# Second mixer: the first pair of groups attended before the compressed blocks, whose part is added later

## The chip, the cores and the metric

One core of a Trainium2 chip runs the whole program. The metric is the device time of one execution in microseconds, and the time of a kernel is the median of its runs. TensorE (PE in the rows) multiplies and transposes, VectorE (DVE) and ScalarE (ACT) work element by element, GpSimd (POOL) does a few small things, and SyncE (SP) issues nearly all transfers. Matmul results land in PSUM, which has eight banks.

## The reference

A decoder trunk of two layers on 256 tokens of width 1024, in fp32. Each layer is a mixer and a SwiGLU FFN, each behind an RMSNorm, with residual additions. The change lies in the second layer's mixer (the "odd" one, native sparse attention): 16 heads of 64 in 4 groups with a key and value head each. Every query gets three attentions, which are gated and added:

```python
s = einsum('bqghd,bngd->bqghn', qb, k_cmp) * scale          # 15 compressed blocks
o_cmp = einsum('bqghn,bngd->bqghd', safe_softmax(s, ...), v_cmp)
...                                                          # o_slc: selected blocks
...                                                          # o_win: sliding window
return g[..., 0:1] * o_cmp + g[..., 1:2] * o_slc + g[..., 2:3] * o_win
```

With 256 tokens there are four selectable blocks and all are selected, and the window of 512 reaches back to the first token, so both o_slc and o_win are causal attentions over all tokens, each with keys and values of its own. The compressed keys and values are made from overlapping stretches of 32 tokens by a small network (`compress`: a matmul over 32 x 64 inputs, a gelu, a second matmul).

## The kernel before

The 256 tokens are two tiles of 128 (t = 0, 1). Every projection is made with three matmuls per 128 rows of weights (`mm3`, lines 264 to 267): a weight tile is split into a rounded part (`w_hi`, ScalarE, line 108) and the rest (`w_lo`, VectorE, line 109), and so are the activations. The class `Weights` loads the tiles in the order of use, five raw buffers and seven split ones, and prepares them six tiles ahead of use. A chunk of w columns (`OD_CHUNKS`) is four weight tiles and 48 matmuls, and its two results take two of the four `mm` banks. The two `s` banks hold scores, and the two `tp` banks hold transposes and the attention's results.

`odd_mixer` works in this order: the chunk of 304 columns (48 gates and the compressed keys' inputs) and that of 256 (the compressed values' inputs), with rope, transposes (`pt_f`) and the sums into `flat` (lines 621 to 667). Then come two pairs of groups (`for gp in range(2)`, line 719), and for each: the queries' chunk of 512, the keys' and values' chunk of 512, their split and transposed forms `qS`, `kS`, `kX`, `vv`; the compressed softmax of both tiles (lines 744 to 768), which ends in `cT`; then for each tile the attention. `compress()` is called once, behind the first queries. The attention of a tile goes in groups: scores into an `s` bank (line 787), maximum and exponential (`softmax_terms`), reciprocal and gate (796, 797), scaling (801), transposes into a `tp` bank (806), eviction to `pT`. When all eight heads are there, one `tp` bank collects the compressed part (814) and the values (822), and `split` writes it into `oT`. Tile 0 has four groups of four scalings of 128 columns for a pair, tile 1 eight groups of two scalings of 256. The first layer of `compress` reads its weights (`cw1`) from the two `pT` buffers, so that the attention cannot write `pT` before.

`residual` is the output projection: eight weight tiles of 1024 columns, each for both tiles and halves, the last three together at the end. Rows 0 to 511 of the weights belong to the first pair, so that their matmuls can run once the first pair's `oT` is there. A norm gain is loaded by SyncE into the single `gain` tile.

The program's text gives priorities: a scheduler takes on each engine, in a simulated time, the ready instruction that stands first in the text, and the engine then runs that fixed order. `pin` holds some instructions (the SyncE queue among them) in the order of the text.

Of the kernel before, what the change touches and what calls it, by code (L numbers as in the profile page):

```python
# [28 lines left out]
OD_CHUNKS = [304, 256, 512, 512, 512, 512]  # L29
# [91 lines left out]
def trunk(tc, x, w0, w1, sm0, cw, vec, cst, out, dbg=None):  # L121
# [481 lines left out]
    def odd_mixer(nm, goff):  # L603
        aT, rs = nm.aT, nm.rs
        with tc.tile_pool(name="odd", bufs=1, reuse_waits="tile") as pool:

            def early(name):
                return pool.tile([P, D], F32, tag="aT", bufs=2 * NT, name=name)


# [10 lines left out]
            for v in range(2):  # L621
# [4 lines left out]
                ps = project(aT, OD_CHUNKS[v])  # L626
                cw1.append(pool.tile([P, 2 * D], F32, tag="pT", bufs=2, name="cw1"))
                pin(nc.sync.dma_start(cw1[v], cw[:, 2 * v * D : (2 * v + 2) * D]))
                for t in range(NT):
                    o = 0  # L630
                    if v == 0:
                        nrs = small_tile(1, "nrs")
                        gt = gates[t].rearrange("p a b c -> p (a b c)")
                        V.tensor_scalar(nrs, rs[t], -1.0, None, op0=ALU.mult)
                        A.activation(gt, ps[t][:, :48], AF.Exp, scale=nrs)
                        V.tensor_scalar(gt, gt, 1.0, None, op0=ALU.add)
                        V.reciprocal(gt, gt)
                        o = 48
                    nk = nat("nk")[:, :384].rearrange("p (a b d) -> p a b d", a=2, b=3)
                    src = ps[t][:, o : o + 256].rearrange("p (a b d) -> p a b d", a=2, b=2)  # L640
                    if v == 0:
                        for a in range(2):
                            rope(pool, nk[:, a, :2], src[:, a], rs[t], t, 2, 64)
                    else:
                        A.activation(nk[:, :, :2], src, AF.Copy, scale=rs[t])
                    V.tensor_copy(nk[:, :, 2], nk[:, :, 0])
                    pt = t_bank("pt_f").rearrange("p (k c) -> p k c", k=4)
                    for a in range(2):
                        for s in range(2):
                            TE.transpose(pt[:, 2 * a + s], nk[:, a, s : s + 2].rearrange("p b d -> p (b d)"), ident)  # L650
                    evac(F[:64, :, t * P : (t + 1) * P], pt[:64])
                    lo, hi = (1, P) if t == 0 else (0, P)
                    for s in range(2):
                        dst = F[64:].rearrange("p (a b) c -> p a b c", b=2)[:, :, 1 - s, t * P + lo - 1 : t * P + hi - 1]
                        evac(dst, pt[64:].rearrange("p (a b) c -> p a b c", b=2)[:, :, s, lo:hi])
# [12 lines left out]

            def compress():

                hp = s_bank("ps_h")[:, :P]
                for j in range(16):
                    for v in range(2):
                        mmi = TE.matmul(
                            hp[64 * v : 64 * v + 64], fls[v][:, j], cw1[v][:, j * P : (j + 1) * P], start=j == 0, stop=j == 15, skip_group_check=True
                        )
                        if j or v:
                            pin(mmi)
# [29 lines left out]
            oT = new_aT(pool)  # L708

# [9 lines left out]
            for gp in range(2):  # L719
                qS = [pool.tile([P, 8, P], F32R, tag="qS", bufs=3, name="qS") for _ in range(NT)]  # L720
                kS = pool.tile([P, 2, 2, T], F32R, tag="kS", bufs=2, name="kS")
                kX = pool.tile([P, 2, 2, T], F32R, tag="kX", bufs=2, name="kX")
                vv = pool.tile([P, NT, 256], F32, tag="vv", bufs=2, name="vv")
                ps = project(aT, 512)
                for t in range(NT):
                    nq = nat("nq").rearrange("p (b d) -> p b d", d=64)
                    rope(pool, nq, ps[t].rearrange("p (b d) -> p b d", d=64), rs[t], t, 8, 64)
                    for h0 in (0, 4):
                        evac(qS[t][:, h0 : h0 + 4], stacked(nq[:, h0 : h0 + 4], 4, "pt_q"))
                if gp == 0:  # L730
                    compress()
                ps = project(aT, 512)
                for t in range(NT):
                    nk = nat("nk")[:, :256].rearrange("p (b d) -> p b d", d=64)
                    rope(pool, nk, ps[t][:, :256].rearrange("p (b d) -> p b d", d=64), rs[t], t, 4, 64)
                    A.activation(vv[:, t], ps[t][:, 256:], AF.Copy, scale=rs[t])
                    pt = stacked(nk, 4, "pt_k").rearrange("p (b r) c -> p r b c", b=2)
                    tq = slice(t * P, (t + 1) * P)
                    evac(kS[:, :, :, tq], pt)
                    for z in range(2):  # L740
                        evac(kX[64 * z : 64 * z + 64, :, :, tq], pt[64 * (1 - z) : 64 * (1 - z) + 64])


                cTs = []
                for t in range(NT):
                    sb = s_bank("ps_c")[:, :256].rearrange("p (h z n) -> p h z n", h=8, z=2)
                    for h in range(8):
                        TE.matmul(sb[:, h].rearrange("p z n -> p (z n)"), qS[t][:, h], kcs[:, 2 * gp + h % 2].rearrange("p z n -> p (z n)"), start=True, stop=True)
                    sc = pool.tile([P, 8, 16], F32, tag="sc", bufs=1, name="sc")
                    mx = small_tile(8, "mx", 2)  # L750
                    dn = small_tile(8, "dn", 2)
                    cm = con[:, C_CMP + 16 * t : C_CMP + 16 * t + 16]
                    V.tensor_add(sc, sb[:, :, 0], cm.unsqueeze(1).broadcast_to([P, 8, 16]))
                    V.tensor_add(sc, sb[:, :, 1], sc)
                    V.tensor_reduce(mx, sc, axis=AX.X, op=ALU.max)
                    V.tensor_scalar(mx, mx, NEG / 10, None, op0=ALU.max)
                    V.tensor_tensor(sc, sc, mx.unsqueeze(2).broadcast_to([P, 8, 16]), op=ALU.subtract)
                    A.activation(sc, sc, AF.Exp, scale=64 ** -0.5)
                    V.tensor_reduce(dn, sc, axis=AX.X, op=ALU.add)
                    V.scalar_tensor_tensor(dn, dn, 0.0, dn, op0=ALU.is_equal, op1=ALU.add)  # L760
                    V.reciprocal(dn, dn)
# [207 lines left out]
```

## Time and profile before

| | us |
|---|---|
| median of 3 runs | 676.5 |
| lowest and highest run | 675.41, 676.85 |
| the profiled execution | 676.92 |
| its span, first to last instruction | 675.1 |
| TensorE busy | 651.3 (96%) |
| VectorE busy | 435.6 (65%) |
| ScalarE busy | 369.5 (55%) |
| mean DMA rate | 162 GB/s |

Times in rows are microseconds from the start of the span. A matmul's row lasts longer than the distance to the next, since matmuls are pipelined: the distance between starts is what one costs in a stream. A bracket at the end of a row tells how long the engine was idle before it and on what it had waited.

### The profile page before, as it was taken

To read this page: it belongs to the slowest core of one execution; us is meant where nothing else is said; L and a number is where in the kernel's file an instruction comes from. 1 tells how busy PE (TensorE), PEld (TensorE's weight loads), DVE (VectorE), ACT (ScalarE), POOL (GpSimd) and SP (SyncE) were. 2 spreads that over 40 slices of the span, in tenths; PEclk is the share of its full clock that TensorE was granted. 3 is DMA by queue.
4 is the path that set the end of the run, shared out by engine and by line. 5 is a ranking of instruction groups with operands and counts; after the bars stand their busy time and mean duration, and the time that the engine had idled before them with its cause. 6 is when DMAs were issued, how large, how long until landed. Compare 5 with 4: busy or idle time off the path is not lost.

```text
span 675.1 us, 9324 instructions
## 1 busy us (share of the span) xinstructions
PE 651.3 (96%) x3329; PEld 533.7 (79%) x3329; DVE 435.6 (65%) x954; ACT 369.5 (55%) x671; POOL 12.4 (2%) x24
## 2 busy tenths in 40 slices
PE   5999999999999999999999999969999999999996
PEld 4979788778888889888887877746788888898884
DVE  4989977767455555543588899696674555465424
ACT  4775847547444444433376687686574544444322
POOL 1000000100000000000000000000000000000000
PEclk9999999999999999999999999989999999999999
DMA  8845355138666666662386431400396555555501
GB/s 313 254 149 168 117 165 157 31 109 319 201 184 184 192 182 184 185 193 74 101 346 216 155 126 39 150 0 2 121 329 196 178 178 196 181 182 187 186 1 62
DMA packets 31869, 109.62 MB, mean 162 GB/s; under 512 B 3536, under 2 KB 3792, under 8 KB 31568
## 3 DMA queue, kind: packets, MB, share of 16 engines
q1 hardware_dynamic: 31392, 108.45, 49.5%
q8 instruction: 26, 0.43, 0.3%
q10 hardware_dynamic: 432, 0.59, 0.2%
q14 instruction: 19, 0.16, 0.1%
HBM read 107.98 MB, written 1.05 MB: 161 GB/s over the span
## 4 chain that ended last, share of the span: by engine, by line
PE 82%; ACT 6%; DMA 5%; DVE 4%; issue 2%; POOL 0%; SPq 0%; POOLq 0%; DVEq 0%; ACTq 0%
PE ps_out L265 7%; PE ps_out L267 7%; PE ps_out L266 7%; PE ps_g L267 5%; PE ps_g L266 5%; PE ps_g L265 5%; PE ps_u L266 5%; PE ps_u L267 5%; PE ps_u L265 5%; DMA w_raw<-in_w 5%; PE ps_in L265 4%; PE ps_in L267 4%; PE ps_in L266 4%; PE pt_a L215 3%; PE ps_o L822 2%
## 5 line engine op out<-in xcount | busy, mean ns | idle before, releaser
L109 DVE TENSOR_TENSOR w_lo<-w_raw,w_hi 128x1024 fp32r<-128x1024 f32 (+5 forms) x200 | 234.5, 1180 | 176.6 <-ACT w_hi L108 176.2
L108 ACT ACTIVATE w_hi<-w_raw 128x1024 fp32r<-128x1024 f32 (+5 forms) x200 | 202.9, 1024 | 203.4 <-PE ps_out L267 58.6
L265 PE MATMUL ps_in<-w_hi,aT 128*128 128x512 f32 (+5 forms) x208 | 77.5, 373 | 1.2 <-ACT aT L209 1.2
L267 PE MATMUL ps_in<-w_hi,aT 128*128 128x512 f32 (+5 forms) x208 | 77.2, 373 | 0.0
L266 PE MATMUL ps_in<-w_lo,aT 128*128 128x512 f32 (+5 forms) x208 | 76.7, 370 | 0.0
L265 PE MATMUL ps_g<-w_hi,aT 128*128 128x512 f32 (+1 forms) x192 | 72.4, 377 | 0.0
L267 PE MATMUL ps_g<-w_hi,aT 128*128 128x512 f32 (+1 forms) x192 | 71.8, 376 | 0.0
L266 PE MATMUL ps_g<-w_lo,aT 128*128 128x512 f32 (+1 forms) x192 | 71.7, 373 | 0.0
L265 PE MATMUL ps_u<-w_hi,aT 128*128 128x512 f32 (+1 forms) x192 | 71.3, 371 | 0.0
L266 PE MATMUL ps_u<-w_lo,aT 128*128 128x512 f32 (+1 forms) x192 | 71.3, 371 | 0.0
L267 PE MATMUL ps_u<-w_hi,aT 128*128 128x512 f32 (+1 forms) x192 | 71.3, 371 | 0.0
L265 PE MATMUL ps_out<-w_hi,hT_hi 128*128 128x512 f32 x176 | 69.5, 395 | 0.0
L267 PE MATMUL ps_out<-w_hi,hT_lo 128*128 128x512 f32 x176 | 69.3, 394 | 0.0
L266 PE MATMUL ps_out<-w_lo,hT_hi 128*128 128x512 f32 x176 | 68.5, 389 | 0.0
L265 PEld LDWEIGHTS ps_in<-w_hi,aT 128*128 128x128 f32 x208 | 39.9, 192 | 6.1 <-ACT aT L209 1.8
L320 ACT ACTIVATE e<-e,bias 128x128 f32<-128x128 f32 (+1 forms) x96 | 42.5, 446 | 3.1 <-DVE bias L319 3.0
L267 PEld LDWEIGHTS ps_in<-w_hi,aT 128*128 128x128 f32 x208 | 39.7, 191 | 4.5 <-DVE aT L210 0.3
L266 PEld LDWEIGHTS ps_in<-w_lo,aT 128*128 128x128 f32 x208 | 39.7, 191 | 4.4 <-issue 0.4
L265 PEld LDWEIGHTS ps_u<-w_hi,aT 128*128 128x128 f32 x192 | 36.2, 188 | 6.3
L266 PEld LDWEIGHTS ps_u<-w_lo,aT 128*128 128x128 f32 x192 | 36.2, 188 | 6.3
L267 PEld LDWEIGHTS ps_u<-w_hi,aT 128*128 128x128 f32 x192 | 36.2, 188 | 6.2
L265 PEld LDWEIGHTS ps_g<-w_hi,aT 128*128 128x128 f32 x192 | 36.2, 188 | 6.0
(208 smaller groups left out, 946.2 us busy)
## 6 DMA issues: line engine op xcount, KB each, us to landing
w_raw<-in_w SPq DMA_DIRECT2D x176, 512.0 KB, 3.6
w_raw<-in_w SPq DMA_DIRECT2D x8, 384.0 KB, 4.6
gain<-in_vec SPq DMA_DIRECT2D x4, 512.0 KB, 5.1
cw<-in_cw SPq DMA_DIRECT2D x2, 1024.0 KB, 8.2
w_raw<-in_w SPq DMA_DIRECT2D x4, 416.0 KB, 6.6
w_raw<-in_w SPq DMA_DIRECT2D x4, 328.0 KB, 6.9
w_raw<-in_w SPq DMA_DIRECT2D x4, 304.0 KB, 2.8
x<-in_x SPq DMA_DIRECT2D x4, 256.0 KB, 6.2
```

The source lines that it names most:

```text
L108: nc.scalar.activation(hi[:, :n], raw[:, :n], AF.Copy)
L109: nc.vector.tensor_sub(lo[:, :n], raw[:, :n], hi[:, :n])
L215: TE.transpose(pt[:, i], src[:, i * P : (i + 1) * P], ident)
L265: TE.matmul(ps, act[0][:, k], wh, start=start, stop=False)
L266: TE.matmul(ps, act[0][:, k], wl, start=False, stop=False)
L267: TE.matmul(ps, act[1][:, k], wh, start=False, stop=stop)
L320: A.activation(e, e, AF.Exp, scale=-1.0, bias=bias, accum_out=den)
L822: pin(TE.matmul(ob[64 * par : 64 * par + 64], vv[:, st, c : c + 64], pTs[par][:, b, st].rearrange("p j c -> p (j c)"), start=False, stop=l ...
```

## The change

The order of the second mixer's program is changed. The first pair's queries, keys and values are projected first. Then the chunk of 304 columns follows (`compress_inputs(0)`, with the gates), then the first pair's attention of tile 0 without its compressed part, the chunk of 256 (`compress_inputs(1)`), and the attention of tile 1. The two results are evicted to SBUF by ScalarE, into the tile of the norm gain. Then come `compress`, and for each tile the first pair's compressed softmax, its product with the compressed values in a bank of its own, an addition on VectorE and the split into `oT`. The second pair is as before. `cw1` lies in four pieces in a third `qS`, a second `kS` and `kX` and an `aT` buffer, no longer in `pT`. In tile 0 the four scalings of a group become one multiplication with a repeated operand, and in tile 1 the gate is a second factor in the scaling, so that the product of reciprocal and gate falls away. The columns on the host are reordered to match.

```diff
-OD_CHUNKS = [304, 256, 512, 512, 512, 512]
+OD_CHUNKS = [512, 512, 304, 256, 512, 512]
...
+            def compress_inputs(v):
                 F = early("F").rearrange("p (g c) -> p g c", g=4)
...
-                ps = project(aT, OD_CHUNKS[v])
-                cw1.append(pool.tile([P, 2 * D], F32, tag="pT", bufs=2, name="cw1"))
-                pin(nc.sync.dma_start(cw1[v], cw[:, 2 * v * D : (2 * v + 2) * D]))
+                ps = project(aT, OD_CHUNKS[2 + v])
+                if v == 0:
+                    tags = (("qS", 3), ("kS", 2), ("kX", 2), ("aT", 2 * NT))
+                    for i, (tag, bufs) in enumerate(tags):
+                        cw1.append(pool.tile([P, D], F32, tag=tag, bufs=bufs, name="cw1"))
+                        pin(nc.sync.dma_start(cw1[i], cw[:, i * D : (i + 1) * D]))
...
-                            cf = den[:, : 2 * g].rearrange("p (g b) -> p g b", b=2)
-                            h0 = 2 * j0 + par
-                            V.reciprocal(cf, cf)
-                            V.tensor_mul(cf, cf, gates[t][:, gp, h0 : h0 + 2 * g - 1 : 2, 1:3])
-                            for i in range(g):
-                                for b in range(2):
-                                    z = 2 * i + b
-                                    V.tensor_scalar(e[:, i, b], e[:, i, b], den[:, z : z + 1], None, op0=ALU.mult)
+                        h0 = 2 * j0 + par
+                        V.reciprocal(den[:, : 2 * g], den[:, : 2 * g])
+                        if t:
+                            for b in range(2):
+                                V.tensor_scalar(e[:, 0, b], e[:, 0, b], den[:, b : b + 1], gates[t][:, p.gp, h0, 1 + b : 2 + b], op0=ALU.mult, op1=ALU.mult)
+                        else:
+                            cf = den.rearrange("p (g b) -> p g b", b=2)
+                            V.tensor_mul(cf, cf, gates[t][:, p.gp, h0 : h0 + 2 * g - 1 : 2, 1:3])
+                            V.tensor_mul(e, e, cf.unsqueeze(3).broadcast_to([P, g, 2, ns]))
...
+            def store(p, t, src):
+                o4 = src.rearrange("p (k c) -> p k c", k=4)
+                k = slice(4 * p.gp, 4 * p.gp + 4)
+                split(oT[t][0][:, k], oT[t][1][:, k], o4)
+
+
+            p0 = inputs(0)
+            compress_inputs(0)
+            o_sw = ap.tile([P, D], F32, tag="gain", bufs=1, name="o_sw")
+            os_ = [o_sw[:, 512 * t : 512 * t + 512] for t in range(NT)]
+            for t in range(NT):
+                pTs = weights(p0, t)
+                ob = t_bank("ps_o")
+                values(ob, p0, t, pTs, True)
+                evac(os_[t], ob)
+                if t == 0:
+                    compress_inputs(1)
+            compress()
+            oT = new_aT(pool)
+            for t in range(NT):
+                cT = compressed(p0, t)
+                ob = t_bank("ps_oc")
+                add_compressed(ob, p0, cT, True)
+                V.tensor_add(os_[t], ob, os_[t])
+                store(p0, t, os_[t])
+            p1 = inputs(1)
+            cTs = [compressed(p1, t) for t in range(NT)]
+            for t in range(NT):
+                pTs = weights(p1, t)
+                ob = t_bank("ps_o")
+                add_compressed(ob, p1, cTs[t], False)
+                values(ob, p1, t, pTs, False)
+                store(p1, t, ob)
```

`inputs`, `compressed`, `weights`, `add_compressed` and `values` hold the lines that stood in the loop over pairs; `gates_of` holds those of the gates.

## Rows read from the trace of the kernel before

**Rows 1.** The page, busy tenths in 40 slices of 16.9 us, TensorE.
```profile
PE   5999999999999999999999999969999999999996
```

**Rows 2.** Table by stage: length, then busy time (and instructions) by engine, granted clock.
```profile
333.00:481.00 148.00, 140.95 (x809) 108.50 (x807) 120.79 (x426) 104.12 (x264) 1.18 (x4) 0.98 0.35 122
437.00:460.00 23.00, 17.11 (x83) 11.35 (x82) 19.27 (x102) 17.73 (x61) 0.00 (x0) 0.85 0.07 23
450.00:456.00 6.00, 4.31 (x18) 3.14 (x19) 5.34 (x25) 3.49 (x12) 0.00 (x0) 0.53 0.00 0
333.00:445.00 112.00, 108.34 (x649) 86.40 (x648) 94.26 (x326) 81.66 (x198) 0.72 (x3) 1.00 0.46 161
333.00:372.00 39.00, 38.13 (x265) 32.65 (x264) 32.25 (x74) 25.67 (x44) 0.72 (x3) 1.00 0.69 259
372.00:426.00 54.00, 53.71 (x288) 41.67 (x288) 49.26 (x192) 40.91 (x114) 0.00 (x0) 1.00 0.38 122
```

**Rows 3.** TensorE's timeline in the second pair's attention: start, duration, instruction, idle before.
```profile
444.83 0.30 PE L765 MATMUL pt_c<-con,sc 128*128 128x128 f32 x1 [2.37 <-DVE sc L763]
444.96 0.60 PE L806 MATMUL pt_p<-con,e 128*128 128x128 f32 x4
...
452.38 0.45 PE L806 MATMUL pt_p<-con,e 128*128 128x128 f32 x1 [1.69 <-DVE e L801]
...
458.01 0.66 PE L806 MATMUL pt_p<-con,e 128*128 128x128 f32 x4
```

**Rows 4.** TensorE's timeline, last transposes and values of tile 0, first pair.
```profile
404.91 0.49 PE L806 MATMUL pt_p<-con,e 128*128 128x128 f32 x3
...
408.81 0.66 PE L806 MATMUL pt_p<-con,e 128*128 128x128 f32 x4
```

**Rows 5.** TensorE's timeline from compression to the end of the first pair's attention.
```profile
361.25 3.68 PE L674 MATMUL ps_h<-cw,flat 128*64 128x128 f32 x62 [0.52 <-issue]
...
384.16 0.29 PE L787 MATMUL ps_s<-kS,qS 128*128 128x256 f32 x1
...
391.16 0.33 PE L765 MATMUL pt_c<-con,sc 128*128 128x128 f32 x1
...
398.72 0.27 PE L765 MATMUL pt_c<-con,sc 128*128 128x128 f32 x1
398.82 0.60 PE L806 MATMUL pt_p<-con,e 128*128 128x128 f32 x4
...
428.52 0.66 PE L716 MATMUL pt_q<-con,stk 128*128 128x128 f32 x4
```

**Rows 6.** VectorE's timeline, the last scalings of a first group, by pair.
```profile
391.81 0.28 DVE L801 TENSOR_SCALAR e<-e,den 128x128 f32<-128x128 f32 x1
...
442.23 0.48 DVE L801 TENSOR_SCALAR e<-e,den 128x128 f32<-128x128 f32 x2
```

**Rows 7.** TensorE's timeline, output projection before the second pair, and the next FFN.
```profile
418.46 0.39 PE L265 MATMUL ps_out<-w_hi,aT 128*128 128x512 f32 x1
418.69 0.39 PE L266 MATMUL ps_out<-w_lo,aT 128*128 128x512 f32 x1
...
441.06 0.40 PE L267 MATMUL ps_out<-w_hi,aT 128*128 128x512 f32 x1
...
480.86 0.40 PE L265 MATMUL ps_g<-w_hi,aT 128*128 128x512 f32 x1
```

**Rows 8.** VectorE's timeline, a product of 512 columns and four scalings of 128.
```profile
403.72 0.69 DVE L315 TENSOR_TENSOR nq<-nq,rope_b 128x512 f32<-128x512 f32 x1
404.32 0.87 DVE L801 TENSOR_SCALAR e<-e,den 128x128 f32<-128x128 f32 x4
```

**Rows 9.** VectorE's groups by form: line, operation, shapes, count, busy us, mean ns.
```profile
L801 DVE TENSOR_SCALAR e<-e,den 128x256 f32<-128x256 f32 x32 | 9.7, 349 | 0.2
L797 DVE TENSOR_TENSOR den<-den,gates 128x2 f32<-128x2 f32 x16 | 2.4, 156 | 0.2
L452 DVE TENSOR_SCALAR am<-iw 128x256 f32<-128x256 f32 x1 | 0.3, 271 | 0.0
```

More of the change, by code (lines that the diff above doesn't have):

```diff
@@ L619, in odd_mixer, with early @@
             cw1 = []
-            for v in range(2):
+            def early(name):
+                return pool.tile([P, D], F32, tag="aT", bufs=2 * NT, name=name)
+            def compress_inputs(v):
                 F = early("F").rearrange("p (g c) -> p g c", g=4)
@@ L648, in odd_mixer @@
                     for a in range(2):
[L649 to L650 removed]
+                        for z in range(2):
+                            TE.transpose(pt[:, 2 * a + z], nk[:, a, z : z + 2].rearrange("p b d -> p (b d)"), ident)
                     evac(F[:64, :, t * P : (t + 1) * P], pt[:64])
                     lo, hi = (1, P) if t == 0 else (0, P)
[L653 to L655 removed]
+                    for z in range(2):
+                        dst = F[64:].rearrange("p (a b) c -> p a b c", b=2)[:, :, 1 - z, t * P + lo - 1 : t * P + hi - 1]
+                        evac(dst, pt[64:].rearrange("p (a b) c -> p a b c", b=2)[:, :, z, lo:hi])
                 for gr in range(4):
@@ L667, in odd_mixer, with gates_of @@
                         )
+            def gates_of(t, src):
+                nrs = small_tile(1, "nrs")
+                gt = gates[t].rearrange("p a b c -> p (a b c)")
+                V.tensor_scalar(nrs, rs[t], -1.0, None, op0=ALU.mult)
+                A.activation(gt, src[:, :48], AF.Exp, scale=nrs)
+                V.tensor_scalar(gt, gt, 1.0, None, op0=ALU.add)
+                V.reciprocal(gt, gt)
             def compress():
@@ L717, in stacked, with inputs @@
                 return pt
[L719 to L723, printed above, removed]
+            class Pair:
+                pass
+            def inputs(gp):
+                h = Pair()
+                h.gp = gp
+                h.qS = [pool.tile([P, 8, P], F32R, tag="qS", bufs=3, name="qS") for _ in range(NT)]
+                h.kS = pool.tile([P, 2, 2, T], F32R, tag="kS", bufs=2, name="kS")
+                h.kX = pool.tile([P, 2, 2, T], F32R, tag="kX", bufs=2, name="kX")
+                h.vv = pool.tile([P, NT, 256], F32, tag="vv", bufs=2, name="vv")
                 ps = project(aT, 512)
@@ L740, in odd_mixer @@
                     for z in range(2):
[L741 to L761, printed above, removed]
-                    V.tensor_mul(dn, dn, gates[t][:, gp, :, 0])
-                    V.tensor_mul(sc, sc, dn.unsqueeze(2).broadcast_to([P, 8, 16]))
-                    pt = t_bank("pt_c")
-                    TE.transpose(pt[:, :P], sc.rearrange("p h n -> p (h n)"), ident)
-                    cT = pool.tile([P, P], F32, tag="cT", bufs=2, name="cT")
-                    evac(cT, pt[:, :P])
-                    cTs.append(cT)
@@ new lines, in values @@
+            def values(ob, p, t, pTs, start):
+                first = True
+                for st in range(t + 1):
+                    for b in range(2):
+                        for par in range(2):
+                            c = b * P + 64 * par
+                            mmi = TE.matmul(
+                                ob[64 * par : 64 * par + 64], p.vv[:, st, c : c + 64], pTs[par][:, b, st].rearrange("p j c -> p (j c)"),
+                                start=start and st == 0 and b == 0, stop=st == t and b == 1, skip_group_check=True,
+                            )
+                            if not (start and first):
+                                pin(mmi)
+                            first = False
@@ L857, in odd_columns @@
     r = lambda a, n: list(range(a, a + n))
-    cols = [2560 + 3 * h + b for gp in range(2) for h in odd_heads(gp) for b in range(3)]
-    cols += r(1024, 512)
+    cols = []
     for gp in range(2):
+        if gp == 1:
+            cols += [2560 + 3 * h + b for g in range(2) for h in odd_heads(g) for b in range(3)] + r(1024, 512)
         for h in odd_heads(gp):
```

136 lines of the change are left out of this document (73 added, 63 removed).

## The prediction

> **What bounds the kernel now.** The page comes first: of TensorE's 40 slices all are 9 tenths busy or more but the first, the last and one in the second mixer, which falls to 6 [rows 1]. So only that place can give time back by reordering. The table by stage comes next [rows 2]. From 333 to 481 us, the second mixer with its output projection, TensorE is busy for 140.95 of 148 us, so it is idle for 7.05, and 23 - 17.11 = 5.89 of these lie between 437 and 460. In the stretch from 450 to 456 the granted clock is 0.53 of full, close to the lower level of 1.2 GHz, after the idle time before it. The timeline of TensorE prices that: the first query tile of the second pair (four transposes, eight matmuls of the compressed part, eight of values) takes from 452.38 to 458.01, 5.63 us; the same work of the first pair took from 404.91 to 408.81, 3.90 us [rows 3, 4]. So 1.73 us go to the slow clock, and at most 7.05 + 1.73 = 8.8 us can be had in this stretch unless work disappears. The order puts no TensorE work out of the kernel: the matmuls are the same in number and shape.
>
> Why the hole is there takes two readings. First, the filler. While attention waits for VectorE and ScalarE, TensorE runs whatever projection is ready. The first pair's attention had both projections of the second pair and then, from 418.46 on, 20 matmuls of the output projection; the second pair's attention has only what is left of that, and from 441.06 on nothing [rows 7]. Second, the transpose banks (two, shared by all transposes) go round in program order. The first pair's weights were scaled at 391.81 + 0.28 = 392.1, yet their transposes run at 398.82, right behind the second transpose of the compressed softmax at 398.72 [rows 5, 6]. In the second pair the scaled weights are there at 442.23 + 0.48 = 442.7 and are transposed at 444.96, again right behind a compressed transpose that waited 2.37 us for VectorE [rows 3, 6]. So what stands earlier in the program holds up what stands later in it, on banks if not on engines.
>
> **The change, part by part.** *Moved order.* The first pair's two projections come first, then the gates and compressed keys, the first pair's attention, the compressed values inside it, then compression, the first pair's compressed softmax, and the second pair. The first pair's attention thus no longer stands behind compression and the compressed softmax. It has as filler the 304- and 256-column chunks and the compression matmuls besides the second pair's projections, so that the 20 matmuls of the output projection (first at 418.46, next at 418.69, so 0.23 us each, 4.6 us) [rows 7] stay for the second pair. The second pair's attention is the last chain before the end of the mixer either way: its first transposes of weights were at 444.96 and the first matmul of the next FFN at 480.86, 35.9 us later [rows 3, 7].
>
> How much earlier can that chain start? What stands before it is VectorE's: 94.26 us of work between 333 and 445, in 112 us [rows 2]. In the opening, 333 to 372, VectorE did 32.25 us in 39; there it waits for projections, and it will do so again, with queries and keys in place of compressed inputs. From 372 to 426 it did 49.26 us in 54, a rate of 0.912, the best that the mixer shows. I let the opening stand and give all that remains the rate of 0.912: (94.26 - 32.25) / 0.912 = 68.0, so the second pair's first transposes come at 333 + 39 + 68 = 440.0 in place of 444.96, 5.0 us earlier. Its ends: if the rate stays at the old mean (94.26 in 112) nothing is won, 0; if VectorE is never late, TensorE's own 8.8 us are the cap. Then the tail: with more filler in it TensorE is not idle long enough to fall to the low clock, which gives the 1.73 us back (ends 0 and 1.73; I take all of it, since the filler of 4.6 us is near the 5.89 us of idle time).
>
> *Scaling, first query tile.* Eight groups (four a pair) replace four scalings of 128 columns, 0.87 us together, by one multiplication of 512 with a repeated operand. The nearest row is a tensor product of 512 columns, 0.69 us [rows 8]: 8 x (0.69 - 0.87) = -1.4 us of VectorE. The Trainium skill speaks against this edit (VectorE: DVE Perf Modes, section on why `tensor_tensor` can't do 2x_2P or 4x): an fp32 product of two tensors gets one element a cycle where a scaling gets two, so each element would cost double. As an estimate by that rule alone, four scalings of 128 would go from about 0.28 us of streaming to 0.56, and the edit would cost 8 x 0.28 = 2.2 us; the trace has the whole duration of both kinds, and the fixed part of three instructions saved outweighs it.
>
> *Scaling, second query tile.* Sixteen products of reciprocal and gate, 0.156 us each, fall away (-2.5 us), and 32 scalings of 256 columns, 0.349 us, get a second per-row factor. The trace has none with two; one with none takes 0.271 us [rows 9], so a per-row factor costs at most 0.078 us, and 32 x 0.078 = +2.5 us; at least 0. I take the upper end, because it is measured for the first factor.
>
> *Added.* Two additions of 128x512 on VectorE, 2 x 0.69 = +1.4 us, and two evictions on ScalarE, which is busy for 104.12 of 148 us and has room [rows 2, 8]. VectorE's sum: -1.4 - 2.5 + 2.5 + 1.4 = 0.0, with the other end at -2.5. So the 94.26 us above stand as they are.
>
> *Buffers and queues.* The compression weights move to four other tiles, in four transfers with the same bytes; they are first needed after the first pair's scores, and behind them in SyncE's queue stand weight tiles that are prepared six ahead. Cost 0. The first pair's output lies in the tile of the norm gain until the second addition; the gain's load will wait for that addition, at about 420, with the last output weights and FFN weights queued behind it. These are wanted from the end of the mixer's attention on, so some 40 us cover it. If the cover were gone, each weight tile late would cost its own 12 matmuls of 0.23 us, 2.8 us.
>
> *Waits added.* Compression's matmuls share two score banks with the first pair's scores, and their transpose stands behind the first pair's values. Behind them stand the first pair's two stores, and behind these the output projection's filler. In the kernel before, this chain (361.25 to the first and second compressed transpose at 391.16 and 398.72, 30 and 37 us) was hidden by projections [rows 5]; in the new one only the second pair's projections cover it.
>
> **Sum.** 5.0 + 1.73 = 6.7 us. The profiled execution took 676.92 us (span 675.1, 1.8 outside it), 0.4 above the median of 676.5. So 676.9 - 6.7 = 670.2 for it, and 669.8 against the median. About 1.35 us, 0.2%, is what a measurement here can tell from no change.
>
> **The rivals.** *Forecast (0.55)*: the hole closes for the most part; 667.5 (all of 8.8) to 673.5. *Half of it (0.15)*: the second pair starts 1 to 3 us earlier, since VectorE is at 0.9 already and its order is only permuted; the clock still falls. 676.5 - 1.4 to 676.5 - 3, so 673.5 to 675.1. For it: VectorE's work isn't reduced; against: it was idle for 6.75 us in the opening and 4.74 us from 372 to 426. *The hole moves (0.13)*: TensorE finishes the second pair's projections and then waits for the first pair's stores as long as it waited before; within 1.35 us of 676.5. This is also the case where the change does not do what it says: the banks' order keeps the attention where it was. *Slower (0.17)*: the chain of compression is exposed. The projections and the first pair's attention keep TensorE busy until about 419 (before, the output projection began at 418.46, when all projections were done [rows 7]). The first store must be there by then. If compression starts at about 385, when the first pair's last scores have left their banks, the first compressed transpose comes 30 us later at 415 and the store at about 417: just in time. If it starts only with the end of that attention (44 us in the kernel before, from its first scores at 384.16 to the end of its values at 428.52 [rows 5]; its first scores now come behind two projections of 48 matmuls, 2 x 11 us, and most of the gates' chunk, some 7 us by its columns, at about 363, so it ends at about 407), the store comes at 439 and TensorE waits for 20 us less the transposes and scores of the second pair. It decides from a first store at about 426 on: each us beyond 419 takes one from the gain of 6.7. At 430 the time is 676.5 + 4.3 = 680.8, the price I give it; 678 to 686.
>
> **How the numbers follow.** The likeliest is the forecast, 669.8. Faster by over 0.2%: 0.55 + 0.15 = 0.70; within: 0.13; slower: 0.17. The range takes in the forecast from 667.5, the half and the same, and the near end of the slower case, to 679.0; outside lie some 0.13 of the slower case and 0.03 below.
>
> **What would show it.** Right: between 437 and 470 TensorE's table has no stretch under 0.9 busy and no clock under 0.9; the second pair's first weight transposes start at about 440; output projection matmuls of the first pair's rows start only after 418 and fill the second pair's attention. Scalings: the 512-column product near 0.69 us, the two-factor scaling between 0.349 and 0.43. Wrong: a wait on TensorE for the first pair's stores or for compression between 395 and 430; a clock that falls there; the second pair's attention starting later than 445.

## The result and the profile after

The changed kernel takes 680.12 us (median of 7 runs, 679.08 to 683.99), the kernel before in the same runs 676.5 us. The ratio is 1.0069, 95% interval 1.0048 to 1.0089: slower by 0.7%. The profiled execution lies on the median, with a span of 678.3 us, 3.2 longer than before. The forecast was 669.8 us and the range ended at 679.0, so both failed.

The table by stage (length, busy time and instructions by engine, then granted clock): the second mixer from its first projection matmul to the first matmul of the FFN, and three stretches in it.

```profile
331.30:484.71 153.41, 143.22 (x812) 111.61 (x811) 119.97 (x389) 104.64 (x266) 1.32 (x4) 0.97 0.31 109
420.00:426.00 6.00, 2.29 (x13) 1.57 (x12) 4.81 (x20) 1.43 (x4) 0.00 (x0) 0.98 0.00 0
426.00:432.00 6.00, 4.28 (x19) 3.75 (x19) 3.05 (x10) 1.22 (x3) 0.00 (x0) 0.50 0.00 0
468.00:474.00 6.00, 3.73 (x18) 3.16 (x20) 3.93 (x10) 2.39 (x8) 0.00 (x0) 0.72 0.01 3
```

The old hole, 5.89 us idle between 437 and 460 [rows 2], is gone: in each stretch of 6 us from 438 to 462 TensorE is busy for 5.82 us or more. In its place stand two. From 420 to 432 TensorE is idle for 3.71 + 1.72 us, and in the second half of that the granted clock is 0.50, the lower of its two levels (1.2 GHz). From 468 to 474 it is idle for 2.27 us at a mean of 0.72. The mixer takes 153.41 us. Before, it went from 332.96 to 480.86, 147.90 us (its end in [rows 7]). So the mixer lost 5.5 us. The rest of the program came out 2.3 us shorter in this execution, though it is unchanged. That part stays unexplained. The mixer of the variants below, but for the two with fewer weight tiles, began between 331.1 and 332.9.

TensorE's timeline of the same kernel (start, duration, instruction, idle time before it and releaser): the first pair's first scores, its last scores, compression, the end of the first pair's values, the last projection, the compressed transposes, the first output projection, the second pair's first weight transposes, and the wait in the second hole.

```profile
363.44 0.28 PE L800 MATMUL ps_s<-kS,qS 128*128 128x256 f32 x1
...
399.45 0.40 PE L800 MATMUL ps_s<-kX,qS 128*128 128x512 f32 x1
...
400.92 1.96 PE L677 MATMUL ps_h<-cw,flat 128*64 128x128 f32 x30
...
412.94 0.59 PE L833 MATMUL ps_o<-pT,vv 128*64 128x512 f32 x1
...
420.83 0.39 PE L267 MATMUL ps_in<-w_hi,aT 128*128 128x512 f32 x1
424.56 0.30 PE L770 MATMUL pt_c<-con,sc 128*128 128x128 f32 x1 [3.34 <-DVE sc L768]
...
428.52 0.48 PE L770 MATMUL pt_c<-con,sc 128*128 128x128 f32 x1 [1.72 <-DVE sc L768]
428.65 0.78 PE L265 MATMUL ps_out<-w_hi,aT 128*128 128x512 f32 x1
...
447.10 0.60 PE L820 MATMUL pt_p<-con,e 128*128 128x128 f32 x4
...
469.84 0.87 PE L820 MATMUL pt_p<-con,e 128*128 128x128 f32 x4 [2.19 <-DVE e L811]
```

The last projection matmul runs at 420.83, the first of the output projection at 428.65. Between them TensorE has only the first pair's compressed chain, and its two long waits there are for `sc`, the weights of the compressed softmax. VectorE's timeline of the same kernel, with one row of ScalarE (ACT), shows why there are two:

```profile
424.12 0.29 DVE L768 TENSOR_TENSOR sc<-sc,dn 128x128 f32<-128x128 f32 x1
424.89 0.29 DVE L758 TENSOR_TENSOR sc<-ps_c,con 128x128 f32<-128x128 f32 x1 [0.48 <-PE pt_c L770]
...
427.15 0.68 DVE L864 TENSOR_TENSOR o_sw<-ps_oc,o_sw 128x512 f32<-128x512 f32 x1
...
427.86 0.63 ACT L209 ACTIVATE aT<-o_sw 128x512 fp32r<-128x512 f32 x1 [1.16 <-DVE o_sw L864]
...
428.53 0.69 DVE L210 TENSOR_TENSOR aT<-o_sw,aT 128x512 fp32r<-128x512 f32 x1
```

The second tile's first addition (424.89) waits until TensorE has transposed the first tile's weights (424.56 + 0.30). There is one `sc` buffer, so the two softmaxes run one behind the other. The first store of the first pair's output is the split into `aT`: ScalarE writes the rounded part by 427.86 + 0.63 = 428.49, VectorE the rest from 428.53. The first output projection matmul (428.65) reads the rounded part and starts 0.16 us after it is written.

The scalings, VectorE's groups by form (count, busy us, mean ns):

```profile
L811 DVE TENSOR_SCALAR e<-e,den,gates 128x256 f32<-128x256 f32 x32 | 11.7, 410 | 0.1
L815 DVE TENSOR_TENSOR e<-e,den 128x512 f32<-128x512 f32 x8 | 5.4, 682 | 0.0
L864 DVE TENSOR_TENSOR o_sw<-ps_oc,o_sw 128x512 f32<-128x512 f32 x2 | 1.4, 687 | 2.4 <-PE ps_oc L777 2.4
```

### The profile page after: what moved, and what is told of

The parts are those of the page before. It is cut to its first block, busy times and chain, and to the rows that moved or that the text cites. A ratio compares the mean times of both kernels' runs of the same rounds, so it can differ in the third digit from the quotient of the medians.

```text
span 678.3 us, 9284 instructions
## 1 busy us (share of the span) xinstructions
PE 652.5 (96%) x3329; PEld 536.4 (79%) x3329; DVE 436.3 (64%) x916; ACT 372.1 (55%) x673; POOL 12.1 (2%) x24
## 4 chain that ended last, share of the span: by engine, by line
PE 84%; DVE 6%; ACT 5%; issue 2%; DMA 2%; POOL 1%; SPq 0%; POOLq 0%; DVEq 0%; ACTq 0%
PE ps_out L266 7%; PE ps_out L265 7%; PE ps_out L267 7%; PE ps_g L267 6%; PE ps_g L265 6%; PE ps_g L266 6%; PE ps_u L267 6%; PE ps_u L266 6%; PE ps_u L265 6%; PE ps_in L265 5%; PE ps_in L267 5%; PE ps_in L266 5%; PE pt_a L215 3%; PE ps_o L833 2%; DMA w_raw<-in_w 2%
```

## Experiments

The runs vary four things: the order, the scaling steps, the number of `sc` buffers, and the place or presence of the first pair's compressed part. Three theories stand at the start. A: the order loses, because the compression starts too late, behind the attention's scores, and its chain is exposed. B: the new scaling makes VectorE later. C: the compressed softmaxes go one behind the other through the single `sc`, with no projection beside them. Each ratio below is against the kernel before, run on the same chip with it. "The mixer" is the time from the first projection matmul to the first of the FFN, as in the table above, from one profiled execution of each kernel. Where two variants were run on different chips, their ratios are the safer comparison.

**Scaling alone.** The old order with the new scaling steps.

```diff
...
-    V.tensor_mul(cf, cf, gates[t][:, gp, h0 : h0 + 2 * g - 1 : 2, 1:3])
-    for i in range(g):
-        for b in range(2):
...
-            V.tensor_scalar(e[:, i, b], e[:, i, b], den[:, z : z + 1], None, op0=ALU.mult)
+    if t:
+        for b in range(2):
+            V.tensor_scalar(e[:, 0, b], e[:, 0, b], den[:, b : b + 1], gates[t][:, gp, h0, 1 + b : 2 + b], op0=ALU.mult, op1=ALU.mult)
+    else:
+        cf = den.rearrange("p (g b) -> p g b", b=2)
+        V.tensor_mul(cf, cf, gates[t][:, gp, h0 : h0 + 2 * g - 1 : 2, 1:3])
+        V.tensor_mul(e, e, cf.unsqueeze(3).broadcast_to([P, g, 2, ns]))
```

> The old order with the new scaling alone. In the changed kernel the 512-column product takes 0.682 us in place of four scalings of 0.87 together, and the scaling with two factors 0.410 in place of 0.349. So VectorE's own sum is 8 x (0.68 - 0.87) + 32 x 0.061 - 16 x 0.156 = -2.0 us of busy time, and the chain of a group of tile 1 loses one step of 0.2 us. Theory A (the loss is the order's: compression stands behind the first pair's attention, and its chain is exposed): this kernel is within 1.4 us of the kernel before or up to 2 us faster, with the old hole between 437 and 460 in place. Rival B (the new scaling makes VectorE later): 678 to 680, with no hole at 420.

Measured: 673.94 us, ratio 0.9972 (0.9961 to 0.9983), the mixer 146.12 us. The edit is a gain of 1.9 us by the ratio, so it isn't what made the changed kernel slow, and theory B falls. The hole of before stays, as the table by stage of this run shows:

```profile
438.00:450.00 12.00, 7.76 (x35) 5.79 (x34) 11.41 (x55) 10.02 (x36) 0.00 (x0) 0.77 0.00 0
```

**Order alone.** The changed kernel with the old scaling steps (the diff above, backwards).

> The new order with the old scaling. Theory A: as slow as the changed kernel or a little slower, 679.5 to 682, with TensorE idle from about 421 on before the first pair's stores and the granted clock at about a half behind it. Rival B: back at 676 to 677.

Measured: 685.89 us, ratio 1.0144 (1.0118 to 1.0170), the mixer 159.42 us. The order alone costs 9.7 us by the ratio, more than theory A had expected (679.5 to 682). TensorE's waits in the mixer (us in total, times, longest):

```profile
PE pt_c L770 <- DVE sc L768: 7.5, 2, 6.0
PE pt_p L819 <- DVE e L814: 5.1, 4, 2.2
```

Both are waits for VectorE. In the changed kernel they are 5.1 and 3.6. The cheaper scaling takes 6.0 us off the mixer in the new order (159.42 to 153.41) and 1.8 in the old (147.90 to 146.12), about three times as much.

**Compression earlier.** The changed kernel with `compress()` ahead of the first pair's second tile.

```diff
                 if t == 0:
                     compress_inputs(1)
-            compress()
+                    compress()
```

> The changed kernel with the call of compression moved ahead of the first pair's attention of tile 1, so that its bank of scores and its transpose come before those of that tile. Theory A: compression's matmuls start at about 393 in place of 401, its transpose comes well ahead of 413, the first store comes before 421, and the wait of 3.3 us on the first compressed transpose goes with the low clock behind it: 672 to 677. Rival C (one buffer for the compressed scores and VectorE's load make the chain long wherever it starts): the first store moves by less than 3 us, and the time is within 1.4 us of the changed kernel.

Measured: 681.49 us, ratio 1.0083 (1.0061 to 1.0106). TensorE's timeline of this run:

```profile
395.26 3.68 PE L677 MATMUL ps_h<-cw,flat 128*64 128x128 f32 x62 [0.26 <-issue]
...
421.85 5.06 PE L833 MATMUL ps_o<-pT,vv 128*64 128x512 f32 x16
426.85 0.33 PE L770 MATMUL pt_c<-con,sc 128*128 128x128 f32 x1
```

Compression, but for two of its 64 matmuls, begins 5.7 us earlier and its own transpose (`pt_h`) comes 9.7 us earlier (403.75 against 413.47). But the compressed transpose comes at 426.85, later than the 424.56 of the changed kernel: it now runs right behind the first pair's values, and those have been pushed back. The rounded part of the first store is written at 430.32, against 428.49. Theory A in its plain form falls: starting the compression earlier did not bring the store earlier.

**A second `sc` buffer** in the changed kernel.

```diff
-                sc = pool.tile([P, 8, 16], F32, tag="sc", bufs=1, name="sc")
+                sc = pool.tile([P, 8, 16], F32, tag="sc", bufs=2, name="sc")
```

> The changed kernel with two buffers for the compressed scores in place of one, so that tile 1's softmax need not wait for tile 0's transpose. Theory A: the first wait (3.3 us on the first compressed transpose) stays, the second (1.7 us) goes, and the clock still falls: 677.5 to 680. Rival C: most of the hole goes, 674 to 677.

Measured: 673.55 us, ratio 0.9974 (0.9962 to 0.9987), 6.6 us under the changed kernel. TensorE's timeline, VectorE's and the table by stage of this run:

```profile
423.82 0.30 PE L770 MATMUL pt_c<-con,sc 128*128 128x128 f32 x1 [2.74 <-DVE dn L765]
426.08 0.42 PE L770 MATMUL pt_c<-con,sc 128*128 128x128 f32 x1
```

```profile
417.35 0.29 DVE L758 TENSOR_TENSOR sc<-ps_c,con 128x128 f32<-128x128 f32 x1 [0.16 <-PE ps_c L753]
418.24 0.29 DVE L758 TENSOR_TENSOR sc<-ps_c,con 128x128 f32<-128x128 f32 x1 [0.60 <-PE ps_c L753]
```

```profile
331.20:478.12 146.92, 141.26 (x812) 109.83 (x811) 118.73 (x389) 104.27 (x266) 1.29 (x4) 0.99 0.33 114
420.00:432.00 12.00, 8.52 (x47) 6.84 (x45) 9.28 (x32) 4.74 (x12) 0.00 (x0) 0.86 0.01 2
```

The two softmaxes now start 0.89 us apart, and the second transpose waits for nothing. The hole at 468 is gone too (5.89 of 6 us busy). The one at 420 has shrunk from 5.43 to 3.48 us of idle time, with the first wait, 2.74 us, left over as theory A had said. The time is a little below C's 674 to 677: C holds for the wait that went. It doesn't say that the new order is good, though: the kernel before has the same single buffer.

**The second buffer in the old order**, as the rival to that: the same one-word edit in the kernel before.

> The kernel before with two buffers for the tile `sc` of the compressed softmax in place of one, and nothing else. Theory C as the second buffer made it (the changed kernel loses because the compressed softmaxes of a pair go through one `sc` one behind the other, and the new order has no projection to run meanwhile): in the old order that chain of the first pair lies beside projections, so the second buffer gains little, 674 to 676 us. Rival D (the one buffer is a fault of the old order just as much, since the second pair's transpose waits 2.37 us on `sc` there too): as much as in the changed kernel less what the scaling hides, 669 to 672 us.

Measured: 668.06 us, ratio 0.9887 (0.9858 to 0.9916), the mixer 140.20 us. Theory C expected 674 to 676 and rival D 669 to 672: D it is, and by more than it asked. The kernel before, VectorE's timeline in both pairs, and TensorE's transpose between the two additions of the second pair:

```profile
391.61 0.28 DVE L753 TENSOR_TENSOR sc<-ps_c,con 128x128 f32<-128x128 f32 x1
...
432.04 0.29 DVE L753 TENSOR_TENSOR sc<-ps_c,con 128x128 f32<-128x128 f32 x1
...
440.48 0.08 DVE L319 DVE_READ_ACCUMULATOR2_ANT bias<- 128x1 f32 x1
440.56 0.29 DVE L753 TENSOR_TENSOR sc<-ps_c,con 128x128 f32<-128x128 f32 x1
```

```profile
440.20 0.33 PE L765 MATMUL pt_c<-con,sc 128*128 128x128 f32 x1
```

The same with two buffers, VectorE in the second pair, TensorE in both, and its table by stage:

```profile
424.57 0.29 DVE L753 TENSOR_TENSOR sc<-ps_c,con 128x128 f32<-128x128 f32 x1 [0.29 <-PE ps_c L748]
...
427.93 0.28 DVE L753 TENSOR_TENSOR sc<-ps_c,con 128x128 f32<-128x128 f32 x1
```

```profile
387.73 0.27 PE L765 MATMUL pt_c<-con,sc 128*128 128x128 f32 x1
...
390.39 0.30 PE L765 MATMUL pt_c<-con,sc 128*128 128x128 f32 x1
...
391.01 0.38 PE L806 MATMUL pt_p<-con,e 128*128 128x128 f32 x2
...
432.88 0.33 PE L765 MATMUL pt_c<-con,sc 128*128 128x128 f32 x1
433.46 0.30 PE L765 MATMUL pt_c<-con,sc 128*128 128x128 f32 x1
434.54 0.27 PE L806 MATMUL pt_p<-con,e 128*128 128x128 f32 x1
```

```profile
437.00:460.00 23.00, 21.13 (x114) 15.67 (x113) 21.38 (x87) 18.87 (x59) 0.00 (x0) 1.00 0.07 24
331.71:471.91 140.20, 137.28 (x812) 108.44 (x811) 119.10 (x427) 102.95 (x264) 1.31 (x4) 1.00 0.36 128
```

With one buffer the second tile's first addition starts at 440.56, 0.03 us after the end of the first tile's transpose (440.20 + 0.33), and in the first pair at 391.61, 0.12 us after it (391.16 + 0.33) [rows 5]. VectorE was not idle right before 440.56 (its instruction before ends there), so the row tells where the softmax stands in VectorE's order, not a wait; that the buffer put it there is what the run with two shows. With two, the second tile starts 4.95 us before the first tile's transpose. The compressed transposes are 0.58 us apart in place of 4.63, and the second pair's first weight transposes come 102.83 us after the mixer's first matmul, before 112.00 (444.96 - 332.96) [rows 3]. Most of these 9.2 us are won in the first pair: its compressed transposes are 2.66 us apart in place of 7.56, and its first weight transposes come 59.30 us after the mixer's first matmul (391.01 - 331.71) in place of 65.86 (398.82 - 332.96) [rows 5]. So 6.6 us come from a chain that lay beside projections, which theory C took to cost nothing, and 2.6 from the second pair. The hole is nearly closed: 1.87 us idle between 437 and 460, at full clock, where it was 5.89 at 0.85 [rows 2], and 2.92 us idle in the whole mixer, where it was 7.05. The old hole was a matter of 512 bytes a partition.

**Scaling and buffer in the old order**, both edits together.

> The kernel before with the new scaling steps and two `sc` buffers, in the old order. Beside the changed kernel with two buffers (673.6 us) it prices the order alone. Theory C: the order's own gain is there once the chain is short, so the old order is 1 to 3 us behind, 674 to 676 us. Rival D: the order is worth nothing or less; 668 to 673 us, and the stretch from 437 to 460 has the hole no more.

Measured: 667.31 us, ratio 0.9872 (0.9845 to 0.9899), the fastest of all and faster than both kernels. The mixer takes 140.44 us. Beside the changed kernel with two buffers, which differs from it in the order alone, it is 6.2 us faster at the medians (on two chips) and 6.5 us in the mixer: the order costs, where theory C expected it to gain 1 to 3. Whether the scaling still helps beside the second buffer (667.31 against 668.06, mixer 140.44 against 140.20) these runs can't tell. Table by stage of this run:

```profile
331.12:471.56 140.44, 137.48 (x812) 108.91 (x811) 118.69 (x387) 103.11 (x264) 1.31 (x4) 1.00 0.36 128
```

Here the output projection takes over from the last projection without a gap (421.88 and 422.11, 0.23 us between starts): the first pair's second store was written by 421.86, its first 18 us earlier.

**Order and buffer** with the old scaling.

> The new order with the old scaling steps and two `sc` buffers: completes the table of order, scaling and buffer. If the three are independent of each other: 685.9 - 6.5 = 679.4 us. If the scaling gains in the new order what it does because VectorE is the releaser there (685.9 to 681.0 = 4.9 with one buffer, 1.9 in the old order), a shorter chain leaves it less to gain: 675 to 678 us. The waits of transposes for `sc` fall from 7.5 us to under 4.

Measured: 679.76 us, ratio 1.0062 (1.0042 to 1.0083), the mixer 152.43 us. With the old scaling, buffer and order add up: 685.9 - 6.5 = 679.4 was expected if they did. The expected smaller gain of the scaling did not show, and the wait for the compressed softmax fell to 5.5 us only, not under 4. With it the table is whole, the mixer in us:

| | one `sc` | two `sc` |
|---|---|---|
| old order, old scaling | 147.90 | 140.20 |
| old order, new scaling | 146.12 | 140.44 |
| new order, old scaling | 159.42 | 152.43 |
| new order, new scaling | 153.41 | 146.92 |

The order costs 11.5, 7.3, 12.2 and 6.5 us; the buffer gains 7.7, 5.7, 7.0 and 6.5; the new scaling gains 1.8 and -0.2 in the old order, 6.0 and 5.5 in the new. So order and scaling do not add up: each depends on the other. The 5.5 us that the changed kernel's mixer lost are the order's 7.3 less the scaling's 1.8.

**Compression earlier, with two buffers.** The edits of the third and fourth run together.

> The changed kernel with two `sc` buffers and the compression called ahead of the first pair's second query tile. Theory A in its rest (compression late, seen only once the buffer is out of the way): 1 to 3 us better than 673.6, so 670.5 to 672.5 us, first compressed transpose before 420. Theory C: the earlier compression stays behind the values in the order of the banks, as it did with one buffer (681.5 against 681.0 expected of none): within 1.35 us of 673.6.

Measured: 674.13 us, ratio 0.9971 (0.9956 to 0.9985), as against 0.9974 without the earlier call; the mixer 147.25 us as against 146.92. Theory A is out in both forms. TensorE's timeline of this run shows what took the hole's place:

```profile
411.16 0.40 PE L267 MATMUL ps_in<-w_hi,aT 128*128 128x512 f32 x1
...
413.81 1.31 PE L820 MATMUL pt_p<-con,e 128*128 128x128 f32 x8 [1.24 <-DVE e L811]
...
425.43 0.33 PE L770 MATMUL pt_c<-con,sc 128*128 128x128 f32 x1
```

The compressed transpose no longer waits for VectorE, but the last projection runs at 411.16 in place of 420.68 with two buffers alone, and TensorE now waits behind it for the scalings of the first pair's attention. Read so, what is exposed is whatever VectorE has left of the first pair when the projections end, and not the compressed chain alone.

**The compressed part after the second pair's inputs.** The question is now why the order still costs 6 us with two buffers. Theory E: when the projections are used up, nothing but the first pair's compressed chain is left for TensorE. Rival F: the loss is elsewhere, in VectorE's share or in the second pair. `inputs(1)` was moved ahead of it, with more `qS` buffers and fewer raw weight tiles, and a control has the fewer raw tiles alone.

```diff
+            p1 = inputs(1)
             oT = new_aT(pool)
             for t in range(NT):
                 cT = compressed(p0, t)
...
-            p1 = inputs(1)
```

> The changed kernel with two `sc` buffers and the second pair's queries, keys and values (`inputs(1)`) set in the program ahead of the first pair's compressed softmax, so that their transposes no longer stand behind it on the banks and can run while it is computed. For that `qS` has five buffers in place of three, and the raw weight tiles three in place of five, to make room. Theory E (the order loses because the first pair's compressed chain has no TensorE work beside it once the projections are used up at 420.7): the stretch from 420 to 430, where TensorE is busy 6.5 of 10 us at a clock of 0.83, is filled, 3 to 5 us come back, 668.5 to 671 us. Rival F (the loss is elsewhere, in VectorE's share or in the second pair): the idle time moves to 430 to 445 and the time stays within 1.35 us of 673.6.

> The control for that: the changed kernel with two `sc` buffers and three raw weight tiles in place of five, nothing else. If the raw tiles are prepared early enough all the same: within 1.35 us of 673.6. If fewer of them hold TensorE up somewhere in the kernel: 675 us or more, and the run with the later compressed part is to be read against this one.

Measured: 681.51 us, ratio 1.0091 (1.0067 to 1.0116), and for the control 681.50 us, ratio 1.0073 (1.0048 to 1.0097). Fewer raw tiles do hold TensorE up: the control is 8 us slower than with five at the medians, 6.7 by the ratios, and its mixer starts only at 336.16. The first of the two gains nothing against it, but as a price it is inconclusive. What can be read is where the chain went, in VectorE's timeline, TensorE's longest wait and the table by stage of the run with the later part:

```profile
430.41 0.48 DVE L758 TENSOR_TENSOR sc<-ps_c,con 128x128 f32<-128x128 f32 x2
```

```profile
PE pt_k L717 <- DVE stk L210: 2.3, 2, 1.6
```

```profile
430.00:440.00 10.00, 8.14 (x38) 7.59 (x39) 6.20 (x29) 5.42 (x13) 0.00 (x0) 0.56 0.00 1
```

The softmax now comes 13 us later (430.41 against 417.35). Idle time and the low clock came to 430 to 440, as rival F said, but TensorE's longest wait is now for the second pair's keys (`pt_k`), not for `sc` (0.5 us). The transposes did not fill the hole; they wait for VectorE themselves.

**Without the chain.** The changed kernel that leaves out the first pair's compressed softmax, its product and the additions, so that it computes less than the reference.

```diff
             for t in range(NT):
-                cT = compressed(p0, t)
-                ob = t_bank("ps_oc")
-                add_compressed(ob, p0, cT, True)
-                V.tensor_add(os_[t], ob, os_[t])
                 store(p0, t, os_[t])
```

> The changed kernel (one `sc` buffer) that leaves out the first pair's compressed part: its compressed softmax, the matmuls with the compressed values and the two additions are not computed, and the first pair is stored as soon as its values are there. This prices the chain whole. Work that goes: some 4.5 us of TensorE (two tiles of 1.96 / 2 + 1.2 + 0.3 us) and some 8 us of VectorE. Theory E: the hole of 420 to 432 goes with it, 5.1 us of waiting and some 2 us of low clock, so 667 to 670 us. Rival F: only the work that goes comes back, 674 to 677 us.

Measured: 669.37 us, ratio 0.9906 (0.9889 to 0.9923), the mixer 141.58 us, 11.8 less than with the chain. The work left out is 4.5 to 5 us of TensorE, an estimate from the rows after, so about 7 us are what exposing the chain costs. VectorE, too, has 5.9 us less to do in the mixer (114.12 against 119.97), so the run prices the chain whole and doesn't tell its order of steps from its load on VectorE. Table by stage and TensorE's timeline of this run:

```profile
420.00:430.00 10.00, 9.82 (x61) 8.07 (x60) 7.51 (x21) 6.67 (x13) 0.00 (x0) 1.00 0.83 321
...
440.00:450.00 10.00, 6.88 (x33) 4.78 (x35) 7.99 (x38) 6.75 (x25) 0.00 (x0) 0.83 0.00 0
```

```profile
442.73 0.33 PE L770 MATMUL pt_c<-con,sc 128*128 128x128 f32 x1 [3.61 <-DVE sc L768]
```

The stretch at 420 is full, and the old hole is back in its old place, with its wait for the single `sc`. Theory E expected 667 to 670 and F 674 to 677: E holds, in the wider form that the run with the earlier compression gave it. As an estimate it also tells what the change would have been worth had the chain been hidden: 669.4 plus the work left out is about 674, not 670.

## Why the prediction was wrong

Two steps failed: the start of compression at 385, which made the slower case look unlikely, and VectorE's work as the cause of the old hole, from which the gain was worked out.

**The rival came true.** The case "slower", with a chance of 0.17, is what happened: the compressed chain of the first pair is exposed. Its mechanism, its place and the point from which it decides (a first store at about 426) were right: the first store was written at 428.5. That its price (680.8 at 430) lies so near the measured 680.1 is in part luck: it set a loss of 11 us against a gain of 6.7, where the run without the chain puts the loss at 6 to 7 and the gain at about 2. What failed is the step that made it unlikely, "if compression starts at about 385, when the first pair's last scores have left their banks". The last of those scores ran at 399.45 and compression started at 400.92. The attention's start at 363 was right to half a microsecond. But compression uses the same two `s` banks and stands behind all twelve score groups of both tiles, and the last of these run near the end of the attention; 385 was halfway through it. The banks were not the only thing in the way: VectorE wrote the last of the sums (`flat`) that compression reads at 393.5, and called ahead of the second tile's scores it began only at 395.26, but for two matmuls. The working had the other end in hand, an attention that ends at about 407 (it ended at 413), and should have started the chain a few us before that. From there it took 23.6 us to the first compressed transpose, less than the 30 taken from before [rows 5], and the store came 11.5 us later than the 417 of the prediction.

**The cause of the old hole was misread.** "What stands before it is VectorE's" is the step under the gain of 5.0 us, and the runs contradict it. With two `sc` buffers and nothing else the second pair's transposes come 9.2 us earlier, while VectorE does 119.10 us of work in the mixer as against 120.79 in a stretch of equal content before [rows 2]. It was not short of time; its fixed order held the second tile's softmax behind the first tile's transpose in both pairs. The forecast followed the wait in [rows 3] back to `sc` on VectorE, took the engine for the cause, and didn't ask what the first write of that tile had stood behind. The prediction's second reading of the hole was right: the first pair's scaled weights do stand behind the compressed transposes (392.1 against 398.82), and the buffer alone brings their transposes 6.6 us forward. The cap of 8.8 us was near (the buffer alone took 7.6 us by the ratio, 8.3 at the medians), but its two parts were not: of the 7.7 us that the mixer lost, 4.1 were idle time and 3.6 busy time, where the cap had 7.05 and 1.73.

**The start of the second pair's attention.** Forecast 440.0, measured 447.10 (before 444.96); from the mixer's first matmul that is 115.80 us against 112.00. It stands behind the first pair's stores, and behind its own compressed softmax through the one `sc`.

**The low clock.** 1.73 us were to come back. In its place the granted clock is 0.50 between 426 and 432, right behind 3.71 us of idle time, and falls once more at 468 (0.72).

**The filler.** This step was right as far as it went: the output projection starts only at 428.65 and the old hole's place from 437 to 460 is filled, as the forecast had it. But filler kept for later is filler missing earlier. From 420.83 to 428.65 there was none, and the text priced this only inside the rival.

**Scaling.** The product of 512 columns takes 0.682 us (forecast 0.69), so tile 0 gains 8 x (0.87 - 0.682) = 1.5 us. The second factor costs 0.410 - 0.349 = 0.061 us, below the bound of 0.078, so tile 1 gains 2.5 - 32 x 0.061 = 0.5. With 1.4 us of additions VectorE's sum is -0.6, forecast 0.0; by the table by stage VectorE went from 120.79 [rows 2] to 119.97, -0.8. The Trainium skill's rule weighed there (VectorE: DVE Perf Modes, section on why `tensor_tensor` can't do 2x_2P or 4x) would have made tile 0 dearer by the prediction's estimate of 2.2 us, which counts streaming alone; the trace disagrees with that estimate, with 0.682 us in all for the product against 0.87 for four scalings, and whether a product gets one element a cycle these totals don't show. What the prediction missed is that the whole edit was worth something on the path: 1.9 us by the ratio in the old order with one buffer (nothing that shows with two), and 5.5 to 6.0 of the mixer in the new one, where TensorE waits for VectorE's scalings.

**Buffers and queues.** Cost 0, and nothing contradicts it: the gain's load goes out at 434.32 with weight tiles behind it, and no weight tile stands in TensorE's waits in the mixer.

**What stays open.** With two buffers and the new scaling, the new order's mixer is 6.5 us longer than the old one's. Of these 2.7 are idle time (5.66 against 2.96). The other 3.8 are busy time (141.26 against 137.48), which includes matmuls at a granted clock of 0.86 from 420 to 432 and small ones with nothing beside them; how it divides was not measured.

## What to carry to other kernels

When a wait ends with an engine's result, go one step further back: a stage that begins right after another's last read of the same tile may be held by a buffer, even where its engine was not idle, and one more buffer may be worth more than a new order. Look for it in every place where the tile is used, also where filler hides the wait: here most of the gain was in the first pair. A chain that runs hidden beside filler has to be priced again at its new place, with the filler that is left there and from the latest of the things that it stands behind, its shared banks among them. Try the smallest edit that could close the hole (here one more buffer of 512 bytes a partition, which took 1.1% off the time) before the one that moves the program.

## What the runs showed of the hardware

A second per-row factor in a scaling of 128x256 costs 0.061 us (0.410 against 0.349). Three raw weight tiles in place of five cost 8 us at the medians (681.50 against 673.55), 6.7 by the ratios. And the granted clock was 0.50, the lower of its two levels, in the 6 us behind a stretch of 6 us with 3.71 us of idle time (420 to 432 in the changed kernel), and 0.72 in the stretch of the second hole, so that matmuls there took longer besides the idle time.
